# A Mamba/attention trunk on one core: mixer transposes by whole PSUM banks, decay matrices and key-query products for two chunks at once, and a planner that counts a switch between float32r and float32 matmuls

## The chip, the core and the metric

The kernel runs on one core of a Trainium2 chip. The core has a matrix engine (TensorE; PE in the profile, and PEld for its weight loads), a vector engine (VectorE, DVE), a scalar engine (ScalarE, ACT), a general engine (GpSimd, POOL) and a queue engine that mostly starts DMAs (SyncE, SP). Each engine runs its own list of instructions strictly in order and waits for the others through semaphores. Matmuls write to PSUM, eight banks of 512 float32 per partition; GpSimd does not read it here, so results leave PSUM through ACT or DVE.

The metric is the device time of one launch in microseconds (us).

## What is computed

Two layers of a diffusion trunk: a Mamba-2 style mixer (SSD scan, forward and backward) and an attention mixer, over 256 context tokens and 1024 latent tokens, all in float32. The change touches the first mixer only. For each of 8 groups g (4 heads each) and each chunk of 128 tokens it computes, cut to what matters:

```
states = jnp.einsum('bcsgn,bcsgr,bcsgrp->bcgrpn', bc, to_end, xc)        # per chunk, then a scan over chunks
seg    = la_cum[:, :, :, None] - la_cum[:, :, None, :]
decay  = jnp.exp(jnp.where(causal, seg, -jnp.inf))
cb     = jnp.einsum('bclgn,bcsgn->bclsg', cc, bc)                        # key-query product of a chunk
w      = cb[..., None] * decay * dtc[:, :, None]
y_diag = jnp.einsum('bclsgr,bcsgrp->bclgrp', w, xc)
y_off  = jnp.einsum('bclgn,bcgrpn,bclgr->bclgrp', cc, prev, jnp.exp(la_cum))
```

with `xc`, `bc`, `cc` the outputs of an input projection, a 5-tap convolution over tokens and a silu.

## The kernel before

The program has three parts one after another: the mixer (to about 1024 us), the mixer's output projection with the second layer's input projection, and attention. Each part has its own `Plan`: while the program is built, every piece of work is put down with `plan.op(engine, function, after, rank, us, takes, uses)`, and `Plan.order` then plays a list schedule with the written durations `us`. On each engine it starts the ready piece with the lowest rank. The result fixes the order of instructions on every engine; on the chip nothing is reordered. `LINK` (0.5 us) is added when a result goes to another engine. `takes`/`uses` are places in rings of buffers: a piece that takes a place can start when one of the ring's buffers is free in the plan. On the chip the buffers of a ring are handed out in turn, so an instruction waits for the oldest one, whichever the plan had in mind. A piece can name a `table`; a piece whose table differs from the engine's last one gets a penalty on its rank and an extra time. Before, only ACT pieces of the first part name one ("exp", "silu"; changing it loads a function table).

**Projections.** 48 column tiles of 128 (32 for the convolution, 16 for the gate z) over 1280 tokens. For each tile, `load` brings two halves of the weights (`wraw`, SP) and splits them into `whi` (ACT, L599) and `wlo` (POOL or DVE in turn, L602), both float32r. `project` multiplies by blocks of 256, 512 and 512 tokens and 8 steps of 128 rows each; a step is three matmuls into a bank `pj` (helper `mm3`, L168 to L170). `pj` has two banks. `conv_tile` copies them to `ub` (ACT, L636), runs five taps over 1282 tokens (ACT L642, DVE L645 four times, 1.8 us each) and the silu (ACT L650). `z_tile` writes silu(z) (L660) to memory. The tiles go in the order of `ORDER`, each with a rank 10 higher than the one before.

**Mixer of a group** (`mix(g, ...)`, called once the group's four tiles x0, x1, B, C are planned, rank 1 above the last of them, rising by 0.01 per piece). All its matmuls are plain float32.
- `trans`, for each of ten chunks: three transposes (x0, x1, B; L690) into one bank `tc`, of which 384 columns are used; x is copied to `xst` by ACT (L695) or DVE (L697), B to `Bt` by ACT (L701). The ring `tc` has two banks.
- `state`, nine steps: for both directions POOL scales x (`xw`, L713) and PE multiplies it with B into the only bank `st` (L718); POOL decays the state (`tm`, L732), DVE adds (`PV`, L736).
- `wmat`, ten chunks: for both directions SP brings a row of cumulative logs broadcast over partitions (`lab`, 3 buffers, L750), POOL masks it (L754), ACT takes four exponentials (L760) into `W0` or `W1` (two buffers each); DVE adds the two (L773); PE makes the key-query product of the chunk into a bank `tc` (L770), with which DVE multiplies (L775). After each second chunk, PE makes the eight diagonal products into `yd` (L795).
- `inner` adds the skip term (DVE L810); `y_out` makes the products with the earlier states (`yo`, one bank, L837), weights them by `es` (DVE L841; `es` comes by DMA, L832), adds (POOL or DVE, L854) and stores `y_d` (L861).

Beside these, `mod_later` works on the modulation of later parts (DVE L902, L923; PE L935, L936, which also takes `tc` banks).

## Time and profile before

| | |
|---|---|
| median of 3 runs | 2016.39 us (2014.74 to 2016.62) |
| profiled execution | 2017.43 us, of which 2015.7 us is the span from the first to the last instruction |
| granted TensorE clock over the span | 0.993 |
| mixer part | the first projection matmul (L168) starts at 72.7 us, the last one at 1023.0 us |
| instructions of the mixer part's `tc` ring | L690 240 transposes, L770 80 products (160 records: a plain float32 matmul shows as two records) |
| ACT function-table loads in the mixer | L760 58, L660 38, L650 26, 1283 ns each |

The profile names an instruction by engine, line and tiles (`tc<-acc`: written tile, then the ones read). "Idle before" is the engine's idle time ahead of an instruction, put down to what ended it. The end of a matmul is modelled, so two matmul records overlap: 512 columns show as 0.39 us but start 0.23 us apart.

### The profile page before, as it was taken

How to read it: one execution, taken by the hardware profiler on the slowest of the kernel's cores; microseconds unless marked ns; L12 is line 12 of the kernel's file. 1: busy time of each engine (PE TensorE's matmuls, PEld its weight loads, DVE VectorE, ACT ScalarE, POOL GpSimd, SP SyncE). 2: the span in 40 equal slices, each digit the busy share in tenths (PEclk: the TensorE clock that was granted, in tenths of full speed). 3: DMA queues.
4: the chain of work that ended last, by engine and by line, in shares of the span. 5: the costliest groups of instructions: out<-in, count | busy, mean ns of one | idle time of the engine just before them, and what ended most of it. 6: DMA issues, size and time to landing. Idle time of an engine off the chain costs nothing.

```text
span 2015.7 us, 30716 instructions
## 1 busy us (share of the span) xinstructions
PE 1953.1 (97%) x10728; PEld 1498.7 (74%) x10728; DVE 1433.2 (71%) x1737; ACT 1119.5 (56%) x2047; POOL 1189.5 (59%) x973
## 2 busy tenths in 40 slices
PE   8899999999999999999999999999999999999998
PEld 8778888888888788888878878887775444444476
DVE  1475897786959686866545888767675888888643
ACT  2446767666766677676734776543224445454521
POOL 1211776666846576856459787754265667776722
PEclk9989999999999999999999999999999999999999
DMA  6114463635373545455486675462233111111033
GB/s 243 63 32 119 133 188 113 187 98 163 113 198 92 150 131 162 142 142 158 147 280 215 216 252 191 156 179 93 76 91 93 32 38 48 43 43 37 6 104 105
DMA packets 163151, 255.51 MB, mean 127 GB/s; under 512 B 22490, under 2 KB 58202, under 8 KB 162996
## 3 DMA queue, kind: packets, MB, share of 16 engines
q1 hardware_dynamic: 161844, 251.71, 41.2%
q8 instruction: 84, 1.38, 0.3%
q10 hardware_dynamic: 1152, 1.84, 0.2%
q14 instruction: 71, 0.58, 0.1%
HBM read 210.78 MB, written 42.63 MB: 126 GB/s over the span
## 4 chain that ended last, share of the span: by engine, by line
PE 73%; DVE 8%; DMA 7%; POOL 3%; ACT 3%; issue 3%; SPq 2%; DVEq 0%; POOLq 0%; ACTq 0%
PE pj L168 8%; PE pj L169 7%; PE pj L170 7%; PE sc L1663 7%; PE ot L1679 7%; PE ob L168 6%; PE ob L170 6%; PE ob L169 6%; DVE acc L645 3%; PE sc L1462 2%; PE yo L837 2%; PE st L718 2%; DMA spare<-in_mod_w 2%; DMA es<-e_d 2%; PE sc L168 1%
## 5 line engine op out<-in xcount | busy, mean ns | idle before, releaser
L168 PE MATMUL pj<-inh,whi 128*128 128x512 f32 (+1 forms) x1152 | 442.0, 384 | 3.1 <-DVE dv L453 2.4
L169 PE MATMUL pj<-inl,whi 128*128 128x512 f32 (+1 forms) x1152 | 410.2, 356 | 0.8 <-POOL inl L367 0.8
L170 PE MATMUL pj<-inh,wlo 128*128 128x512 f32 (+1 forms) x1152 | 411.0, 357 | 0.0
L168 PEld LDWEIGHTS pj<-inh,whi 128*128 128x128 f32 x1152 | 219.2, 190 | 31.4 <-DVE dv L453 2.8
L170 PEld LDWEIGHTS pj<-inh,wlo 128*128 128x128 f32 x1152 | 218.5, 190 | 32.3
L645 DVE SCALAR_TENSOR_TENSOR acc<-ub,convw,acc 128x1282 f32<-128x1282 f32 x128 | 229.4, 1793 | 17.0 <-ACT acc L642 14.0
L169 PEld LDWEIGHTS pj<-inl,whi 128*128 128x128 f32 x1152 | 219.6, 191 | 26.6 <-POOL inl L367 1.2
L760 ACT ACTIVATE W<-lab,u_t 128x128 f32<-128x128 f32 x640 | 202.7, 391 | 64.6 <-POOL lab L754 42.0
L754 POOL TENSOR_SCALAR_AFFINE_SELECT lab<-lab 128x512 f32<-128x512 f32 x160 | 145.6, 915 | 153.5 <-DMA lab<-la_d 108.6
L1644 POOL TENSOR_TENSOR acc<-acc,P 128x1024 f32<-128x1024 f32 x80 | 192.8, 2411 | 64.1 <-ACT P L1668 62.6
L1668 ACT ACTIVATE P<-sc 128x1024 f32<-128x1024 f32 x160 | 162.9, 1025 | 120.0 <-PE sc L1663 104.4
L1609 DVE TENSOR_REDUCE mx<-sc 128x2 f32<-128x1024 f32 (+1 forms) x140 | 167.4, 1213 | 37.3 <-PE sc L1462 36.4
L713 POOL TENSOR_TENSOR xw<-xst,te_t 128x256 f32<-128x256 f32 x144 | 143.0, 1009 | 41.6 <-PE st L718 17.5
L1679 PE MATMUL ot<-P,vv 128*64 128x512 f32 x640 | 154.7, 605 | 0.0
L602 POOL TENSOR_TENSOR wlo<-wraw,whi 128x512 fp32r<-128x512 f32 x48 | 72.1, 1501 | 121.9 <-ACT whi L599 121.7
L1663 PE MATMUL sc<-q,kh 64*128 64x512 f32 x640 | 136.6, 423 | 4.9 <-DVE qs L1375 2.6
L1663 PEld LDWEIGHTS sc<-q,kh 64*128 64x128 f32 x640 | 60.4, 185 | 74.6 <-DVE mx L1609 29.6
L170 PE MATMUL ob<-whi,yl 128*128 128x512 f32 x288 | 113.4, 394 | 1.8 <-DVE yl L1061 1.4
L168 PE MATMUL ob<-whi,yh 128*128 128x512 f32 x288 | 113.9, 395 | 0.0
L169 PE MATMUL ob<-wlo,yh 128*128 128x512 f32 x288 | 113.0, 392 | 0.0
L902 DVE SCALAR_TENSOR_TENSOR macc<-mraw,cc,macc 128x512 f32<-128x512 f32 x98 | 101.2, 1058 | 11.1 <-DMA mraw<-in_mod_w 10.9
L732 POOL TENSOR_TENSOR tm<-PV,dec_t 128x512 f32<-128x512 f32 x64 | 92.5, 1446 | 17.8 <-DVE PV L736 16.7
(281 smaller groups left out, 4501.8 us busy)
## 6 DMA issues: line engine op xcount, KB each, us to landing
lab<-la_d SPq DMA_DIRECT2D x160, 256.0 KB
wraw<-in_w_in SPq DMA_DIRECT2D x96, 256.0 KB
workvv<-in_m_out_w SPq DMA_DIRECT2D x94, 256.0 KB
mraw<-in_mod_w SPq DMA_DIRECT2D x64, 256.0 KB
es<-e_d SPq DMA_DIRECT2D x128, 128.0 KB
wraw<-in_wqkv SPq DMA_DIRECT2D x48, 256.0 KB
spare<-in_mod_w SPq DMA_DIRECT2D x32, 256.0 KB
q_d<-qs SPq DMA_DIRECT2D x128, 64.0 KB
```

The costliest lines, as they stand in the source:

```text
L168: T.matmul(o, lh, rh, start=first, stop=False)
L169: T.matmul(o, lh, rl, start=False, stop=False)
L170: T.matmul(o, ll, rh, start=False, stop=last)
L645: V.scalar_tensor_tensor(t["a"], ub[i % 2][:, k:k + CW], convw[:, ct, k:k + 1], t["a"], op0=OP.mult, op1=OP.add)
L713: G.tensor_tensor(t[d], s["xst"][:, c], te_t[:, d, c, h4][:, :, None].to_broadcast([128, 4, 64]), op=OP.mult)
L754: G.affine_select(t["l", d], t["l", d], [[0, 4], [sgn, 128]], OP.is_ge, NEVER, base=0, channel_multiplier=-sgn)
L760: S.activation(t["w", d][:, h], t["l", d][:, h], AF.Exp, bias=u_t[:, d, c, 4 * g + h:4 * g + h + 1])
L1609: V.tensor_reduce(max_place(t["m"][0], i), o, AX.X, OP.max)
L1644: E.tensor_tensor(t[e], t["P", k0] if two else t[e], t["P", kt], op=OP.add)
L1663: T.matmul(o[:, h], (first_row[r] if n == 3 else (kh, kl, kh)[n][r, kv, k]), x[(0, 0, 1, 2)[n]][r], start=(n == 0), stop=(n == 3))
L1668: S.activation(t["P", kt], flat(t["s", kt]), AF.Exp)
L1679: T.matmul(t["o"][h * 64:(h + 1) * 64], vv[:, kt, kv], t["P", kt][:, h * 512:(h + 1) * 512], start=(kt == 0), stop=(kt == NT - 1))
```

## The change

It has four pieces, all in the first part.

1. **Transposes by whole banks.** `trans` is called five times instead of ten. It transposes x0 and x1 of two chunks into one bank (512 columns) and copies it at once (ACT for three of the five, DVE for two); B is transposed for four chunks into one bank (the last time two) and copied by ACT at once. `xst` and `Bt` hold the chunks in the order of the transposes, and `at[c]` finds them. The transposes of x no longer wait for the tile B.
2. **Two chunks at once in `wmat`.** It is called for every second chunk. Direction 1 goes first, then direction 0, four exponentials per chunk and direction as before. One DVE addition and one DVE multiplication work on 1024 columns; the two key-query products share a `tc` bank, and the plan starts them only after the third set of four exponentials. `W0` and `W1` hold two chunks and have one buffer each, so the memory is the same and there is no second buffer.
3. **Tables for PE.** In this part the projections name the table "parts" and the mixer's matmuls "whole". The plan charges a change with 4 on the rank and 0.08 us (`plan.switch["PE"]`).
4. **Rings in turn.** For rings named in `ROUND` (here `tc`) the plan gives out a place only if the places before it that share its buffer are free, as the chip does.

The number of matmuls, transposes, exponentials, POOL instructions and DMAs is the same. The order of instructions in the two later parts is the same on every engine.

```diff
+ROUND = ("tc", "y")
...
                     if any(self.free[h.ring] <= i or h.ring not in ANY and h.n != self.given.get(h.ring, 0) + i + 1
-                           for h, i in o.takes):
+                           or h.ring in ROUND and any(x.users for x in out[h.ring][:max(0, len(out[h.ring]) + i + 1 - size[h.ring])]) for h, i in o.takes):
                         continue
-                    r = o.rank + (SWITCH[e][0] if o.table and o.table != table.get(e) else 0.)
+                    r = o.rank + (self.switch[e][0] if o.table and o.table != table.get(e) else 0.)
...
-                 "st": 1, "yd": 1, "yo": 1, "xst": 1, "Bt": 1, "PV": 1, "xw": 3, "tm": 1, "lab": NLAB, "W0": 2, "W1": 2, "es": 3})
+                 "st": 1, "yd": 1, "yo": 1, "xst": 1, "Bt": 1, "PV": 1, "xw": 3, "tm": 1, "lab": NLAB, "W0": 1, "W1": 1, "es": 3})
...
-                               .69 if hi - lo > 256 else .36, takes=[bank] if kt == 0 else [], uses=[bank, w[kt // 4][1]])
+                               .69 if hi - lo > 256 else .36, takes=[bank] if kt == 0 else [], uses=[bank, w[kt // 4][1]], table="parts")
...
-        def trans(n, c):
-            t0, bank, t = tok0(c), plan.hold("tc"), {}
-
-            def turn():
-                t["p"] = psum("tc", [128, 3, 128])
-                for j, x in enumerate((x0, x1, bt)):
-                    T.transpose(t["p"][:, j, :], x["a"][:, t0:t0 + 128], ident)
...
+            def turn(key, tiles, cs):
+                t[key] = psum("tc", [128, len(cs), len(tiles), 128])
+                for i, c in enumerate(cs):
+                    for j, x in enumerate(tiles):
+                        T.transpose(t[key][:, i, j, :], x["a"][:, tok0(c):tok0(c) + 128], ident)
+
+            cs, bank = order[2 * n:2 * n + 2], plan.hold("tc")
+            p = op("PE", lambda: turn("x", (x0, x1), cs), [ax0, ax1, s.get("x")] + third, .45, takes=[bank] + ([] if n else [hxst]),
+                   uses=[hx0, hx1, hxst], table="whole")
+
+            s.setdefault("x", p)
...
-                xd = s["xst"][:, c].rearrange("p h d -> p (h d)")
+                o, i = s["xst"][:, 2 * n:2 * n + 2].rearrange("p c h d -> p (c h d)"), t["x"].rearrange("p c x t -> p (c x t)")
                 if n % 2 == 0:
-                    S.activation(xd, flat(t["p"][:, 0:2]), AF.Copy)
+                    S.activation(o, i, AF.Copy)
                 else:
-                    V.tensor_copy(xd, flat(t["p"][:, 0:2]))
-
-            a = op("PE", turn, [ax0, ax1, ab] + third, .33, takes=[bank] + ([hxst, hBt] if n == 0 else []), uses=[hx0, hx1, hb, hxst, hBt])
-            b = op("DVE" if n % 2 else "ACT", xcopy, [a], .42 if n % 2 else .38, uses=[bank, hxst])
-            d = op("ACT", lambda: S.activation(s["Bt"][:, c, :], t["p"][:, 2, :], AF.Copy), [a], .275, uses=[bank, hBt])
-            ready[c] = (b, d)
...
+            xo = op("DVE" if n % 2 else "ACT", xcopy, [p], .68 if n % 2 else .6, uses=[bank, hxst])
+            if n % 2 == 0:
+                cb, bank2 = order[2 * n:2 * n + 4], plan.hold("tc")
+                p = op("PE", lambda: turn("b", (bt,), cb), [ab, s.get("b")] + third, .11 * len(cb), takes=[bank2] + ([] if n else [hBt]),
+                       uses=[hb, hBt], table="whole")
+                s.setdefault("b", p)
+                d = op("ACT", lambda: S.activation(flat(s["Bt"][:, 2 * n:2 * n + len(cb)]), t["b"].rearrange("p c x t -> p (c x t)"),
+                                                   AF.Copy), [p], .15 * len(cb), uses=[bank2, hBt])
+                for c in cb:
+                    ready[c] = [None, d]
+            for c in cs:
+                ready[c][0] = xo
...
-        def wmat(c):
-                def expo(h, d=d):
-                    if h == 0:
-                        t["w", d] = pool["now"].tile([128, 4, 128], FT, tag=f"W{d}", bufs=2, name="W")
-                    S.activation(t["w", d][:, h], t["l", d][:, h], AF.Exp, bias=u_t[:, d, c, 4 * g + h:4 * g + h + 1])
-                a = op("SP", bring, third + [la_op], .38, takes=[hl])
-                a = op("POOL", close, [a], .88, uses=[hl])
-                for h in range(4):
-                    a = op("ACT", lambda h=h, f=expo: f(h), [a, u_op], .312, takes=[hw] if h == 0 else [], uses=[hl, hw], table="exp")
-                ws.append((hw, a))
...
+        def wmat(c0):
+
+            t, bank, hw = {}, plan.hold("tc"), [plan.hold(f"W{d}") for d in range(2)]
+            done, two = [], (c0, c0 + 1)
+            for d in (1, 0):
+                first = None
+                for k, c in enumerate(two):
+                    hl = plan.hold("lab")
...
+                    def expo(h, d=d, k=k, c=c):
+                        if k == 0 and h == 0:
+                            t["w", d] = pool["now"].tile([128, 2, 4, 128], FT, tag=f"W{d}", bufs=1, name="W")
+                        S.activation(t["w", d][:, k, h], t["l", d, k][:, h], AF.Exp, bias=u_t[:, d, c, 4 * g + h:4 * g + h + 1])
+
+                    a = op("SP", bring, third + [la_op], .38, takes=[hl])
+                    a = op("POOL", close, [a], .88, uses=[hl])
+                    for h in range(4):
+                        a = op("ACT", lambda h=h, f=expo: f(h), [a, u_op, first], .312, takes=[hw[d]] if h == k == 0 else [], uses=[hl, hw[d]],
+                               table="exp")
+                    first = a
+                    done.append(a)
...
             def cross():
-                t["cb"] = psum("tc", [128, 128])
-                T.matmul(t["cb"], bt["a"][:, t0:t0 + 128], ct["a"][:, t0:t0 + 128], start=True, stop=True)
-
-            b = op("PE", cross, [ab, ac], .22, takes=[bank], uses=[hb, hc])
-            a = op("DVE", lambda: V.tensor_tensor(t["w", 0], t["w", 0], t["w", 1], op=OP.add), [w[1] for w in ws], .75,
-                   uses=[w[0] for w in ws])
-            a = op("DVE", lambda: V.tensor_tensor(t["w", 0], t["w", 0], t["cb"][:, None, :].to_broadcast([128, 4, 128]),
-                                                  op=OP.mult), [a, b], .68, uses=[ws[0][0], bank])
...
+                t["cb"] = psum("tc", [128, 2, 128])
+                for k, c in enumerate(two):
+                    T.matmul(t["cb"][:, k], bt["a"][:, tok0(c):tok0(c) + 128], ct["a"][:, tok0(c):tok0(c) + 128], start=True, stop=True)
+
+            def weigh():
+                w = t["w", 0]
+                V.tensor_tensor(w, w, t["cb"][:, :, None, :].to_broadcast([128, 2, 4, 128]), op=OP.mult)
+
+            a = op("DVE", lambda: V.tensor_tensor(t["w", 0], t["w", 0], t["w", 1], op=OP.add), done, 1.3, uses=hw)
+            b = op("PE", cross, [ab, ac, done[2]], .44, takes=[bank], uses=[hb, hc], table="whole")
+            a = op("DVE", weigh, [a, b], 1.22, uses=[hw[0], bank])
...
-                for c, t, _, _ in two:
+                for n, c in enumerate(two):
+            bk["ops"].append(op("PE", diag, [a] + [ready[c][0] for c in two], 1.08, takes=[bk["h"]] if new else [],
+                                uses=[bk["h"], hxst, hw[0]], table="whole"))
...
+    plan.switch["PE"] = (4., .08)
```

What this does to the order of instructions is shown at three places. The lines of the changed kernel are other than before: L172 to L174 are the three projection matmuls (before L168 to L170), L701 the transposes (L690), L743 the state products (L718), L802 the key-query products (L770), L825 the diagonal products (L795), L789 the exponentials (L760).

The first place is PE in the mixer of the third group, at its transposes (`tc<-ident,acc`), with state products and projection steps between them; before:

```order
L690 MATMUL tc<-ident,acc 128x128 x3
L718 MATMUL st<-xw,Bt 128x256 x2
L168 MATMUL pj<-inh,whi 128x512
L169 MATMUL pj<-inl,whi 128x512
L170 MATMUL pj<-inh,wlo 128x512
L690 MATMUL tc<-ident,acc 128x128 x3
```

And in the changed kernel, in the same group:

```order
L701 MATMUL tc<-ident,acc 128x128 x8
L172 MATMUL pj<-inh,whi 128x512
L173 MATMUL pj<-inl,whi 128x512
L174 MATMUL pj<-inh,wlo 128x512
L701 MATMUL tc<-ident,acc 128x128 x4
L743 MATMUL st<-xw,Bt 128x256 x2
L701 MATMUL tc<-ident,acc 128x128 x2
```

One run of three transposes filled one bank; now eight fill two banks, and one projection step stands before the next bank is asked for.

The second place is a little later on PE in the same group, at the first key-query products (`tc<-acc`) and the first diagonal products (`yd<-W,xst`); before:

```order
L770 MATMUL tc<-acc 128x128
L718 MATMUL st<-xw,Bt 128x256 x2
L770 MATMUL tc<-acc 128x128
L168 MATMUL pj<-inh,whi 128x512
L169 MATMUL pj<-inl,whi 128x512
L170 MATMUL pj<-inh,wlo 128x512
L795 MATMUL yd<-W,xst 64x128 x8
L770 MATMUL tc<-acc 128x128
```

And in the changed kernel:

```order
L802 MATMUL tc<-acc 128x128 x2
L172 MATMUL pj<-inh,whi 128x512
L173 MATMUL pj<-inl,whi 128x512
L174 MATMUL pj<-inh,wlo 128x512
L172 MATMUL pj<-inh,whi 128x512
L173 MATMUL pj<-inl,whi 128x512
L174 MATMUL pj<-inh,wlo 128x512
L743 MATMUL st<-xw,Bt 128x256 x2
L172 MATMUL pj<-inh,whi 128x512
L173 MATMUL pj<-inl,whi 128x512
L174 MATMUL pj<-inh,wlo 128x512
L825 MATMUL yd<-W,xst 64x128 x8
```

Before, a third product stood right behind the second one's projection step and the diagonal products; now the two products of a pair stand together, and the diagonal products come three projection steps later, with no further product ahead of them.

The third place is ACT about halfway through the mixer, at the exponentials (`W<-lab,u_t`) of the changed kernel, with what they wait for. The first row is the first exponential into `W0` of a pair:

```order
L789 ACTIVATE W<-lab,u_t 128x128 [waits DVE_49,DMAHW3_49,PE_49,Pool_49]
L789 ACTIVATE W<-lab,u_t 128x128 x3
L603 ACTIVATE whi<-wraw 128x512 [waits DMAHW5_49]
L603 ACTIVATE whi<-wraw 128x512 [waits DMAHW7_49,PE_49]
L640 ACTIVATE ub_110<-pj 128x512 [waits PE_49]
L646 ACTIVATE acc<-ub_110,convw 128x1282 [waits Activation_49]
```

The wait for PE in the first row is for the diagonal products of the pair before, which read the only `W0`; the weight splits and the copy out of the projection's bank stand behind it in ACT's queue.

72 lines of the change are left out of this document (36 added, 36 removed).

## The prediction

> **What bounds the kernel now.** I read the page first, for the engine that the end hangs on, then PE's idle time stretch by stretch, and then who ends it.
>
> ```profile
> PE 1953.1 (97%) x10728; PEld 1498.7 (74%) x10728; DVE 1433.2 (71%) x1737; ACT 1119.5 (56%) x2047; POOL 1189.5 (59%) x973
> PE 73%; DVE 8%; DMA 7%; POOL 3%; ACT 3%; issue 3%; SPq 2%; DVEq 0%; POOLq 0%; ACTq 0%
> ```
>
> PE is busy 97% of the span and carries 73% of the chain that ends last; no other engine passes 71%. The change leaves PE's matmuls as many and as large as they were, so it can only win what PE loses by waiting in the mixer. The stretches (us, then PE's busy time first):
>
> ```profile
> 112.00:1008.00 896.00, 878.60 (x5258) 748.53 (x5259) 678.20 (x783) 618.34 (x1231) 535.24 (x474) 1.00 0.48 139
> 600.00:700.00 100.00, 96.30 (x575) 80.92 (x574) 80.22 (x89) 62.03 (x129) 60.12 (x50) 1.00 0.45 125
> 900.00:1008.00 108.00, 107.95 (x675) 93.03 (x674) 63.59 (x86) 77.28 (x151) 58.30 (x62) 1.00 0.51 152
> 1008.00:1060.00 52.00, 49.03 (x227) 39.34 (x227) 25.56 (x25) 19.64 (x35) 30.18 (x23) 1.00 0.86 281
> ```
>
> From 112 to 1008 us PE is idle for 896 − 878.6 = 17.4 us, most of it in the middle (3.7 us of 600 to 700, next to nothing at the end), and 3.0 us at the passage into the next part. PE's own waits between 112 and 1008 us (waiting line, what ended the wait, us, times, longest):
>
> ```profile
> PE tc L770 <- DVE W L775: 4.9, 6, 1.2
> PE st L718 <- POOL xw L713: 4.9, 5, 2.5
> PE yo L837 <- DVE es L841: 3.2, 6, 1.2
> PE pj L168 <- DVE dv L453: 2.4, 1, 2.4
> PE st L718 <- DVE PV L736: 1.8, 3, 1.2
> PE tc L690 <- DVE xst L697: 0.6, 2, 0.4
> PE tc L690 <- ACT mr L939: 0.6, 1, 0.6
> ```
>
> Without the one at L168, ahead of the mixer, that is 16.0 us in 23 waits. A wait costs a little more than its row says, as PE's row of matmuls shows:
>
> ```profile
> 307.86 0.39 PE L170 MATMUL pj<-inh,wlo 128*128 128x512 f32 x1
> 309.11 0.49 PE L770 MATMUL tc<-acc 128*128 128x128 f32 x2 [0.86 <-DVE W L775]
> ...
> 549.21 0.49 PE L770 MATMUL tc<-acc 128*128 128x128 f32 x2 [1.19 <-DVE W L775]
> 549.63 1.09 PE L795 MATMUL yd<-W,xst 128*64 128x128 f32 x16
> ...
> 670.92 0.28 PE L169 MATMUL pj<-inl,whi 128*128 128x256 f32 x1
> 671.04 0.28 PE L170 MATMUL pj<-inh,wlo 128*128 128x256 f32 x1
> 672.32 0.49 PE L770 MATMUL tc<-acc 128*128 128x128 f32 x2 [1.01 <-DVE W L775]
> 672.65 0.39 PE L837 MATMUL yo<-acc,PV 128*128 128x128 f32 x2
> ```
>
> From 307.86 to 309.11 are 1.25 us where 0.23 us is the usual distance (303.32 to 303.55 below): 1.02 us lost for an idle time of 0.86, so 0.16 us more. With 23 × 0.16 = 3.7 us, the mixer loses 19.7 us to waits. With the 3.0 us behind 1008, a gain over some 23 us has no source in this profile.
>
> **The change, term by term.** The sum is made on the profiled execution (2017.43 us, 1.7 us of it around the span).
>
> *Waits for a `tc` bank* (L770 and L690): 4.9 + 0.6 + 0.6 us in 9 waits, with 9 × 0.16 = 7.5 us. PE asks for the oldest bank while DVE still has to multiply from it. The new plan gives banks in turn, half as many products ask for one, and a product starts only after three of four sets of exponentials; these waits should go. But the diagonal products need the same multiplication. At 549.21 they followed at once (0.42 us later), and the wait would have come there in full. At 309.11 a projection step and state products came between, and at 672.32 a `yo` product followed, no diagonal product; there it would be gone. I take 60%: **−4.5 us** (bounds −7.5 and 0).
>
> *State and `yo` products*: 4.9 + 1.8 + 3.2 us in 14 waits, with 2.2 us 12.1 us. They hang on POOL and DVE being late, and POOL's work stays. DVE and ACT get lighter:
>
> ```profile
> L760 ACT ACT_TABLE_LOAD x58 | 74.4, 1283 | 3.2 <-issue 1.1 <-DVE W L773 0.7 <-DVE W L775 0.5
> L773 DVE TENSOR_TENSOR W<-W 128x512 f32<-128x512 f32 x80 | 69.7, 872 | 39.5 <-ACT W L760 39.1
> L775 DVE TENSOR_TENSOR W<-W,tc 128x512 f32<-128x512 f32 x80 | 54.7, 685 | 3.6 <-PE tc L770 1.4
> L841 DVE TENSOR_TENSOR es<-yo,es 128x512 f32<-128x512 f32 x64 | 43.9, 687 | 50.1 <-DMA es<-e_d 24.5 <-PE yo L837 10.6 <-DMA lab<-la_d 3.5
> L701 ACT ACTIVATE Bt<-tc 128x128 f32<-128x128 f32 x80 | 19.8, 276 | 8.8 <-PE tc L690 5.8 <-DVE xst L697 2.9
> L697 DVE COPY xst<-tc 128x256 f32<-128x256 f32 x40 | 16.1, 415 | 12.7 <-PE tc L690 8.3 <-ACT Bt L701 4.2
> L695 ACT ACTIVATE xst<-tc 128x256 f32<-128x256 f32 x40 | 15.2, 379 | 14.5 <-PE tc L690 14.4
> L725 ACT ACTIVATE PV<-st 128x512 f32<-128x512 f32 x8 | 4.8, 600 | 1.2 <-PE st L718 1.2
> L841 DVE TENSOR_TENSOR es<-yo,es 128x128 f32<-128x128 f32 x32 | 9.2, 287 | 17.7 <-PE yo L837 12.6 <-DMA es<-e_d 4.9
> ```
>
> On DVE 128 columns take 287 ns and 512 take 687, so a column costs 1.04 ns and an instruction 0.154 us by itself. 160 instructions of `W` become 80: 12.3 us less. 40 copies of x become 16 of 512 columns: 16.6 − 16 × 0.687 = 5.6 us less. Together 18 of 678 us. On ACT, 40 copies of x and 80 of B (15.2 + 22.1 us at 379 and 276 ns) become 40 of 512 columns at 600 ns (24 and 16) and 8 of 256 at 379: 27.0 us, 10 us less. The order also has 12 table loads fewer: 15.4 us. None of this is on the chain itself; PE's work covers it, and it only makes DVE and ACT less late where PE waits. Some 3% of load moves waits little: **−1.0 us** of the 12.1 (bounds −6 and +6, half of them either way, since every piece gets another place).
>
> *Fewer switches between projections and mixer.* Runs of mixer matmuls between projections fall from 288 to 224 by the order. The products' durations (minimum, median, maximum in ns), and one switch there and back without a wait:
>
> ```profile
> L770 PE MATMUL tc<-acc x160: 270/273/377, 174.8 to 988.1; 128*128 128x128 f32 x160
> ...
> 303.09 0.39 PE L169 MATMUL pj<-inl,whi 128*128 128x512 f32 x1
> 303.32 0.39 PE L170 MATMUL pj<-inh,wlo 128*128 128x512 f32 x1
> 303.55 0.60 PE L770 MATMUL tc<-acc 128*128 128x128 f32 x4
> 303.91 0.48 PE L168 MATMUL pj<-inh,whi 128*128 128x512 f32 x1
> 304.22 0.40 PE L169 MATMUL pj<-inl,whi 128*128 128x512 f32 x1
> ```
>
> From 303.32 to 304.22 are 0.90 us. Two projection matmuls at 0.23 and four records at 0.11 (the four of L770 last 0.60, the last one alone its median of 0.273) make 0.90: a switch costs about 0.01 us. 64 fewer: **−0.8 us** (bounds −1.5 and 0). The rule meant to keep float32 together does hardly more: its penalty is 4 and the next tile's rank is 10 higher, so ready mixer work still goes first.
>
> *The passage at 1008 to 1060.* In the new order 23 projection steps stand behind the last `yo` product, before 15; at 0.69 us a step the mixer's tail ends 5.5 us earlier against PE's end. But the stores of z hang on the last projections. **−0.5 us** of the 3.0 (bounds −3 and +2).
>
> *A plan that thinks PE slower.* It charges 0.08 us for each of some 448 changes, 36 us that PE will not spend, 4% of 896. PE comes to a mixer product earlier than planned; over a lead that I put at 5 us that is 0.2 us for each of 23 waits: **+1.0 us** (bounds 0 and +4.6).
>
> Sum: −4.5 − 1.0 − 0.8 − 0.5 + 1.0 = −5.8, so 2011.6 us against 2017.43. The median shown (2016.39) lies 1.04 us below that execution: **2010.6 us**.
>
> **Rivals.** *Most waits go* (chance 0.12): all 7.5 us at `tc`, half of the 12.1, 0.8 and the 3.0 at the passage, 17 us: 1999 us. For it speaks that from 900 to 1008 us PE already runs without waits at a similar load.
>
> *The waits change places* (0.26): DVE's late multiplication stops PE at L795 instead, as at 549, and POOL's is late as before. 0 to −3 us: 2013 to 2016.
>
> *The wide additions hold up POOL* (0.05).
>
> ```profile
> L773 DVE TENSOR_TENSOR W<-W x80: 672/693/1790, 198.9 to 999.2; 128x512 f32<-128x512 f32 x80
> L713 POOL TENSOR_TENSOR xw<-xst,te_t x144: 603/1042/1889, 204.5 to 964.5; 128x256 f32<-128x256 f32 x144
> ```
>
> The addition (minimum, median, maximum in ns) takes from 672 to 1790 and POOL's scaling from 603 to 1889, while DVE's multiplication from PSUM stays at 685: where DVE and POOL both read SBUF, one waits for the other. An addition of 1024 columns lasts 0.672 + 512 × 1.04 ns = 1.2 us, so POOL waits on average 0.6 us for it instead of 0.34, in half as many places: 40 × 1.2 × 0.6 − 80 × 0.672 × 0.336 = 10.7 us at most, 6 us at POOL's share of 0.6. If all of it reached PE through `xw`, the gain would be used up: 2016 us. The Trainium skill, page "SBUF — State Buffer", section "SBUF: two separate sides", says that such an addition and a GpSimd instruction reading SBUF shut each other out for a whole instruction. The rows just shown agree with that rule.
>
> *The single `W0` blocks ACT* (0.13), the slow side.
>
> ```profile
> ACT W L760 <- PE yd L795: 19.9, 12, 4.7
> ...
> L760 ACT ACTIVATE W<-lab,u_t 128x128 f32<-128x128 f32 x640 | 202.7, 391 | 64.6 <-POOL lab L754 42.0 <-PE yd L795 19.9 <-issue 1.8
> ```
>
> Already with two buffers ACT waits 19.9 us for diagonal products, once 4.7 us. With one, each of 40 pairs waits for the pair before, and behind that exponential ACT's queue holds the copy out of `pj`. A 256-token block takes eight steps of three matmuls at 0.12 us (670.92 to 671.04), 2.9 us; if ACT stands longer than that, PE has no free `pj` bank. Ten such pairs at 1.5 us cost 15 us: 2025 us. Against it: five pairs in a group's 100 us leave 20 us for a chain of some 10 us (16 exponentials at 0.39, 1.2 + 1.2 on DVE, 1.1 on PE).
>
> **How the numbers follow.** The forecast has 0.44 (its own range 2004 to 2014), the rivals 0.12, 0.26, 0.05 and 0.13. Differences under 0.2% (4.0 us) can't be told from no change here. Faster than 2012.4: 0.40 of the forecast and 0.12 = 0.52. Same: 0.04 + 0.24 + 0.04 = 0.32; slower 0.16. The range 1997 to 2022 leaves out the far ends of the fast and the slow rival, some 0.15; its lower end is the fast rival with 2 us more, its upper end lies within the slow one.
>
> **What would show it.** In the profile of the changed kernel: no wait at the key-query products (L802), and shorter new ones at L825; state and `yo` waits near 12 us; table loads 12 fewer; between 112 and 1008 us PE idle near 13 us. Waits at projections (L172) behind ACT's copies would make the slow rival right; PE idle of 17 us with L825 in the list, the second one; and a distance over 0.95 us where 0.90 stands above, a switch dearer than I read it.

## The result and the profile after

| | before | after |
|---|---|---|
| median of six runs each | 2015.97 us (2011.57 to 2018.80) | 2027.63 us (2023.40 to 2028.71) |
| profiled execution, its span | 2017.43, 2015.7 us | 2028.56, 2026.8 us |
| first transpose of the mixer | 202.2 us | 179.0 us |
| last `yo` product | 1013.3 us | 1018.8 us |
| last projection matmul | 1023.4 us | 1033.6 us |

The ratio of the times is 1.0052, 95% interval 1.0038 to 1.0065: the changed kernel is half a per cent slower. 10.2 of the 11.1 us by which its span is longer are there when the last projection is done, so the mixer part is the place. The first group's mixer work starts 23 us earlier and still the last `yo` product comes 5.5 us later.

The page's busy times and chain of the changed kernel:

```profile
PE 1951.7 (96%) x10728; PEld 1500.2 (74%) x10728; DVE 1422.6 (70%) x1633; ACT 1099.0 (54%) x1963; POOL 1204.3 (59%) x973
PE 64%; DVE 8%; DMA 3%; ACT 3%; issue 2%; POOL 1%; SPq 1%; DVEq 0%; ACTq 0%; POOLq 0%
```

PE's busy time is the same within 1.4 us, so the added time is idle time. By stretches (us, then PE, PEld, DVE, ACT and POOL busy, the granted clock, DMA), first of the changed kernel:

```profile
112.00:1008.00 896.00, 867.16 (x5188) 740.12 (x5188) 660.46 (x669) 591.45 (x1137) 550.12 (x473) 0.99 0.48 138
200.00:300.00 100.00, 92.07 (x572) 77.52 (x570) 86.76 (x84) 69.45 (x140) 74.57 (x59) 1.00 0.51 144
300.00:400.00 100.00, 94.35 (x564) 80.61 (x563) 68.22 (x72) 69.09 (x132) 55.66 (x51) 1.00 0.55 154
600.00:700.00 100.00, 96.00 (x575) 81.76 (x574) 77.83 (x78) 62.15 (x125) 67.65 (x55) 0.98 0.46 129
900.00:1008.00 108.00, 107.82 (x669) 92.69 (x668) 64.47 (x71) 74.53 (x142) 67.26 (x64) 1.00 0.55 165
1008.00:1060.00 52.00, 49.45 (x244) 40.73 (x243) 21.97 (x26) 18.08 (x33) 21.46 (x18) 0.97 0.74 247
```

From 112 to 1008 us PE now idles 28.8 us, before 17.4. The stretches where before it hardly waited have become the worst, with 7.9 us idle of 200 to 300 and 5.7 us of 300 to 400 (2.4 and 1.6 us before); at the end it still runs without waits. DVE and ACT give no reason by their busy time, which is lower than before, and the clock gives none either: over the whole span 0.993 was granted in both kernels. PE's own waits in the mixer part (waiting line, what ended the wait, us, times, longest):

```profile
PE st L743 <- DVE PV L762: 13.0, 15, 2.1
PE yo L867 <- DVE es L871: 8.2, 6, 2.5
PE yd L825 <- DVE W L806: 2.8, 5, 1.5
PE tc L701 <- ACT Bt L722: 2.7, 1, 2.7
PE st L743 <- POOL xw L738: 1.1, 2, 0.9
PE tc L802 <- DVE xst L714: 0.7, 1, 0.7
PE st L743 <- ACT PV L751: 0.2, 1, 0.2
```

The waits for a `tc` bank behind DVE's multiplication are gone. PE waits instead behind the state's addition (13.0 us, before 1.8) and the `es` product (8.2, before 3.2), two instructions that the change did not touch. One such wait, in the timeline of all engines (start, length, engine, line):

```profile
208.34 3.21 DVE L932 SCALAR_TENSOR_TENSOR macc<-mraw,cc,macc 128x512 f32<-128x512 f32 x3
...
208.90 1.13 PE L743 MATMUL st<-xw,Bt 128*128 128x256 f32 x4
...
211.48 0.86 DVE L840 SCALAR_TENSOR_TENSOR acc<-acc,dskip,yd 128x256 f32<-128x256 f32 x2
...
211.85 0.28 PE L174 MATMUL pj<-inh,wlo 128*128 128x256 f32 x1
...
212.26 0.67 DVE L762 TENSOR_TENSOR PV<-tm,st 128x512 f32<-128x512 f32 x1
...
212.99 1.13 PE L743 MATMUL st<-xw,Bt 128*128 128x256 f32 x4 [0.85 <-DVE PV L762]
```

The addition that frees the only `st` bank has its place on DVE behind three background updates (3.21 us) and two skip terms. PE is through its four projection steps at 212.1, while DVE, which has not paused since 208.34, gets to the addition only at 212.26. DVE works without a pause while PE stands: in the order this addition has its place too late for a PE of this speed.

### The profile page after: what moved, and what is told of

Read it like the earlier page. It is cut to its first block, busy times and chain, and to the rows that moved or that the text cites. A ratio compares the mean times of both kernels' runs of the same rounds, so it can differ in the third digit from the quotient of the medians.

```text
span 2026.8 us, 30474 instructions
## 1 busy us (share of the span) xinstructions
PE 1951.7 (96%) x10728; PEld 1500.2 (74%) x10728; DVE 1422.6 (70%) x1633; ACT 1099.0 (54%) x1963; POOL 1204.3 (59%) x973
## 4 chain that ended last, share of the span: by engine, by line
PE 64%; DVE 8%; DMA 3%; ACT 3%; issue 2%; POOL 1%; SPq 1%; DVEq 0%; ACTq 0%; POOLq 0%
PE sc L1694 7%; PE ot L1710 7%; PE ob L172 6%; PE ob L174 6%; PE ob L173 6%; PE pj L172 5%; PE pj L173 5%; PE pj L174 5%; DVE acc L649 3%; PE yo L867 2%; PE sc L1493 2%; PE st L743 2%; PE sc L172 1%; PE sc L174 1%; PE sc L173 1%
## 5 line engine op out<-in xcount | busy, mean ns | idle before, releaser
L172 PE MATMUL pj<-inh,whi 128*128 128x512 f32 (+1 forms) x1152 | 436.5, 379 | 3.9 <-DVE dv L457 3.2
L174 PE MATMUL pj<-inh,wlo 128*128 128x512 f32 (+1 forms) x1152 | 410.4, 356 | 0.0
L649 DVE SCALAR_TENSOR_TENSOR acc<-ub,convw,acc 128x1282 f32<-128x1282 f32 x128 | 230.6, 1801 | 18.3 <-ACT acc L646 14.8
L172 PEld LDWEIGHTS pj<-inh,whi 128*128 128x128 f32 x1152 | 219.1, 190 | 32.6 <-DVE dv L457 3.6
L174 PEld LDWEIGHTS pj<-inh,wlo 128*128 128x128 f32 x1152 | 218.3, 190 | 31.9
L789 ACT ACTIVATE W<-lab,u_t 128x128 f32<-128x128 f32 x640 | 202.1, 390 | 61.5 <-POOL lab L783 37.9
L783 POOL TENSOR_SCALAR_AFFINE_SELECT lab<-lab 128x512 f32<-128x512 f32 x160 | 157.7, 992 | 116.3 <-DMA lab<-la_d 99.8
L738 POOL TENSOR_TENSOR xw<-xst,te_t 128x256 f32<-128x256 f32 x144 | 152.4, 1075 | 35.7 <-PE st L743 23.2
L871 DVE TENSOR_TENSOR es<-yo,es 128x512 f32<-128x512 f32 (+1 forms) x96 | 53.1, 553 | 101.1 <-DMA es<-e_d 47.3
L758 POOL TENSOR_TENSOR tm<-PV,dec_t 128x512 f32<-128x512 f32 x64 | 96.8, 1512 | 36.3 <-DVE PV L762 36.2
L174 PE MATMUL ob<-whi,yl 128*128 128x512 f32 x288 | 113.4, 394 | 1.8 <-DVE yl L1092 1.8
L172 PE MATMUL ob<-whi,yh 128*128 128x512 f32 x288 | 114.1, 396 | 0.0
```

The lines of the kernel that those rows point to most:

```text
L172: T.matmul(o, lh, rh, start=first, stop=False)
L174: T.matmul(o, ll, rh, start=False, stop=last)
L649: V.scalar_tensor_tensor(t["a"], ub[i % 2][:, k:k + CW], convw[:, ct, k:k + 1], t["a"], op0=OP.mult, op1=OP.add)
L738: G.tensor_tensor(t[d], s["xst"][:, at[c]], te_t[:, d, c, h4][:, :, None].to_broadcast([128, 4, 64]), op=OP.mult)
L783: G.affine_select(t["l", d, k], t["l", d, k], [[0, 4], [sgn, 128]], OP.is_ge, NEVER, base=0, channel_multiplier=-sgn)
L789: S.activation(t["w", d][:, k, h], t["l", d, k][:, h], AF.Exp, bias=u_t[:, d, c, 4 * g + h:4 * g + h + 1])
```

## The experiments

Four theories stood against each other. **The charge**: the plan reckons with 0.08 us at each change between projections and mixer, the chip needs about 0.01, so the order is made for a slower PE. **The pairs**: two chunks of `W` at once make DVE, ACT and POOL work in larger lumps. **The banks**: transposes by whole banks tie the start of a group to two or four chunks. **Scatter** ("replan" in the expectations): any edit gives another order, and orders differ by some 10 us without a cause. In the expectations the charge is called "price".

To compare orders I add up, from the 300th to the last projection matmul of the mixer, how much longer than usual the step from one matmul to the next is where the trace shows PE idle between them; this is called "waits" below (before 21.1 us in 29 places, after 34.6 in 35). Without its waits that stretch is 848 to 855 us long in every kernel, while the waits go from 8.3 to 34.6 us, so the waits are most of the difference. They are read from one profiled execution of each kernel, and that execution lies up to 5 us off the kernel's median (e7's was its slowest, e8's its fastest). "Runs" are the uninterrupted runs of mixer matmuls between projections, counted in the order. The ratios are against the kernel before, timed again with each set on the same chip; e1 to e4, e5 to e8 and e9 to e12 were each timed together.

| kernel | median us | ratio (95%) | waits us / places | runs |
|---|---|---|---|---|
| after | 2027.63 | 1.0052 (1.0038 to 1.0065) | 34.6 / 35 | 224 |
| e1: after, charge 0 | 2008.98 | 0.9974 (0.9960 to 0.9988) | 17.8 / 25 | 228 |
| e2: after, old `wmat` | 2029.96 | 1.0086 (1.0063 to 1.0108) | 31.2 / 52 | 244 |
| e3: after, old `trans` | 2028.44 | 1.0073 (1.0048 to 1.0099) | 30.2 / 36 | 240 |
| e4: before, rings in turn | 2010.51 | 0.9981 (0.9965 to 0.9998) | 14.8 / 24 | 278 |
| e5: before, tables and charge | 2024.31 | 1.0050 (1.0035 to 1.0065) | 29.8 / 38 | 267 |
| e6: charge 0, steps planned 4.5% longer | 2019.82 | 1.0024 (1.0014 to 1.0034) | 28.9 / 38 | 246 |
| e7: after, charge 0 and penalty 0 | 2009.56 | 0.9977 (0.9968 to 0.9987) | 18.2 / 27 | 257 |
| e8: after, charge 0.01 | 2007.95 | 0.9966 (0.9954 to 0.9977) | 15.1 / 23 | 231 |
| e9: after, all but PE planned 4.5% slower | 2001.76 | 0.9931 (0.9916 to 0.9946) | 11.8 / 19 | 222 |
| e10: charge 0.01, DVE and POOL as measured | 2000.54 | 0.9929 (0.9914 to 0.9944) | 8.3 / 11 | 229 |
| e11: after, charge 0.04 | 2018.69 | 1.0017 (1.0004 to 1.0029) | 25.5 / 30 | 231 |
| e12: e7 without rings in turn | 2013.93 | 0.9996 (0.9984 to 1.0008) | 23.0 / 29 | 259 |

### e1 to e4: which piece

**e1**, the change without its charge:

```diff
-    plan.switch["PE"] = (4., .08)
+    plan.switch["PE"] = (4., 0.)
```

> The changed kernel with one number altered: the plan charges no time for a PE switch between projections and mixer (the rank penalty of 4 stays). Theory 'price' (the plan thinks PE slower by 0.08 us at some 448 switches, so PE reaches the mixer's products earlier than planned and waits there): about 2016 us, PE's waits in the mixer back from 28.7 to some 16 us. Theory 'pairs' (two chunks at once make DVE's state additions and the es loads late): stays at 2024 to 2030 us, with waits of state products for DVE L762 near 13 us and of yo near 8. Theory 'replan' (every new order scatters by some 10 us, whatever the reason for it): anywhere from 2010 to 2030.

Measured 2008.98 us, ratio 0.9974. PE's busy time from 112 to 1008 us and its waits in this kernel:

```profile
112.00:1008.00 896.00, 882.24 (x5319) 754.70 (x5318) 675.77 (x685) 599.68 (x1149) 565.19 (x478) 1.00 0.47 142
```

```profile
PE st L743 <- DVE PV L762: 5.3, 7, 1.5
PE yd L825 <- DVE W L806: 3.3, 6, 1.0
PE yo L867 <- DVE es L871: 1.8, 3, 1.1
PE tc L701 <- DVE xst L714: 1.7, 2, 1.4
PE st L743 <- POOL xw L738: 1.0, 1, 1.0
```

One number, which no instruction of the kernel contains, turns a loss of 0.5% into a gain of 0.3%; the time is 7 us under the 2016 us expected of the charge theory. PE's idle time falls from 28.8 to 13.8 us, and what falls are the waits at the two lines that had grown (13.0 to 5.3 and 8.2 to 1.8).

**e2**, the change with the decay matrices one chunk at a time, as before (two buffers of `W0` and `W1`), and the charge kept:

```diff
-        def wmat(c0):
+        def wmat(c):
...
-            a = op("DVE", lambda: V.tensor_tensor(t["w", 0], t["w", 0], t["w", 1], op=OP.add), done, 1.3, uses=hw)
-            b = op("PE", cross, [ab, ac, done[2]], .44, takes=[bank], uses=[hb, hc], table="whole")
-            a = op("DVE", weigh, [a, b], 1.22, uses=[hw[0], bank])
...
+            b = op("PE", cross, [ab, ac], .22, takes=[bank], uses=[hb, hc], table="whole")
+            a = op("DVE", lambda: V.tensor_tensor(t["w", 0], t["w", 0], t["w", 1], op=OP.add), [w[1] for w in ws], .75,
+                   uses=[w[0] for w in ws])
```

> The changed kernel with the decay matrices one chunk at a time as before (512-column additions and multiplications, two buffers each for W0 and W1, one key-query product per bank); the transposes by whole banks, the PE tables and the rings in turn stay. Theory 'pairs': back to 2013 to 2018 us, waits for DVE L762's state addition and for es under 8 us together. Theory 'price': stays over 2023 us. Theory 'replan': anywhere from 2010 to 2030.

Measured 2029.96 us, ratio 1.0086: the pairs are not the cause. Without them the loss is no smaller, and the waits for a `tc` bank behind DVE's multiplication are back (8.7 us in 12 places).

**e3**, the change with the transposes three per chunk, as before, and the charge kept:

```diff
-        def trans(n):
+        def trans(n, c):
...
+                t["p"] = psum("tc", [128, 3, 128])
+                for j, x in enumerate((x0, x1, bt)):
+                    T.transpose(t["p"][:, j, :], x["a"][:, t0:t0 + 128], ident)
...
-        for n in range(NT // 2):
-            trans(n)
+        for n, c in enumerate(order):
+            trans(n, c)
```

> The changed kernel with the transposes three at a time per chunk as before; the decay matrices for two chunks, the PE tables and the rings in turn stay. Theories 'price' and 'pairs': both 2023 us and more. A theory 'banks' (the transposes by whole banks, and their earlier start, are what costs): about 2016 us. Theory 'replan': anywhere from 2010 to 2030.

Measured 2028.44 us, ratio 1.0073: the banks are not the cause either.

**e4**, the kernel before with the rule on rings alone:

```diff
+ROUND = ("tc", "y")
...
-                           for h, i in o.takes):
+                           or h.ring in ROUND and any(x.users for x in out[h.ring][:max(0, len(out[h.ring]) + i + 1 - size[h.ring])]) for h, i in o.takes):
```

> The kernel before with the rings in turn alone (the plan gives a tc bank only when the older holder of its buffer is done). By the prediction's first term: the 7.5 us of waits for tc banks shrink to 3 or less and the time falls to about 2011 us. Theory 'replan': the waits move to other lines, and the time lies anywhere from 2008 to 2026.

Measured 2010.51 us, ratio 0.9981. The time is as expected, the way there is not: the waits at `tc` are still 5.9 us (before 6.1), and the gain came at the state and `yo` products (4.5 us, before 9.9). A rule on one ring moved the whole order.

### e5 to e8: the charge without the rest, and other ways to a slow PE

**e5**, the kernel before with the tables and the charge alone:

```diff
-                               .69 if hi - lo > 256 else .36, takes=[bank] if kt == 0 else [], uses=[bank, w[kt // 4][1]])
+                               .69 if hi - lo > 256 else .36, takes=[bank] if kt == 0 else [], uses=[bank, w[kt // 4][1]], table="parts")
...
-            b = op("PE", cross, [ab, ac], .22, takes=[bank], uses=[hb, hc])
+            b = op("PE", cross, [ab, ac], .22, takes=[bank], uses=[hb, hc], table="whole")
...
+    plan.switch["PE"] = (4., .08)
```

> The kernel before with the PE tables alone (projections 'parts', mixer 'whole', penalty 4 and 0.08 us per change of table in the plan); transposes, decay matrices and rings as before. Theory 'price': 2024 us or more and 28 us or more of PE waits in the mixer, with nothing else of the change in it. Theory 'replan': anywhere from 2008 to 2030. If it stays at 2010 to 2016 us, 'price' needs another piece of the change to act.

Measured 2024.31 us, ratio 1.0050. PE's waits in it:

```profile
PE tc L771 <- DVE W L776: 8.3, 12, 1.4
PE yo L838 <- DVE es L842: 7.4, 8, 1.8
PE st L719 <- POOL xw L714: 3.5, 5, 0.8
PE st L719 <- DVE PV L737: 3.5, 7, 1.0
PE tc L691 <- ACT Bt L702: 0.6, 1, 0.6
```

The charge costs the old code as much as the whole change does. Three of the four larger waits of before are longer and in more places: 8.3 us in 12 where the product waits for DVE's multiplication, before 4.9 in 6; `yo` 7.4 (3.2 before) and the state's addition 3.5 (1.8). The fourth, for POOL's `xw`, is shorter (3.5, before 4.9). So the charge has no line of its own: in the old code it lengthens other waits than in the changed one.

**e6**, no charge, but each projection step planned at 0.72 us instead of 0.69 (0.375 instead of 0.36 for 256 tokens), which also makes PE about 4% slower in the plan alone:

```diff
-                               .69 if hi - lo > 256 else .36, takes=[bank] if kt == 0 else [], uses=[bank, w[kt // 4][1]], table="parts")
+                               .72 if hi - lo > 256 else .375, takes=[bank] if kt == 0 else [], uses=[bank, w[kt // 4][1]], table="parts")
...
-    plan.switch["PE"] = (4., .08)
+    plan.switch["PE"] = (4., 0.)
```

> The changed kernel with no time for a switch, but with each projection step planned 4% too long (0.72 and 0.375 us for 0.69 and 0.36; the trace has 0.68 and 0.36), some 36 us over the mixer, as much as 448 switches at 0.08. Theory 'price' in its general form (a plan in which PE is slower than on the chip puts products too early for DVE and the es loads): 2022 us or more. If only the switch as such mattered: about 2009, as without its time. Theory 'replan': anywhere from 2005 to 2030.

Measured 2019.82 us, ratio 1.0024. Against e1 it loses 0.5%, and 11 us of waits. The direction is that of the charge theory, but the 2022 us or more that it expected were not reached: the loss against e1 is some two thirds of the charge's.

**e7**, no charge and no penalty, so that the order takes no notice of the two kinds of matmul:

```diff
-    plan.switch["PE"] = (4., .08)
+    plan.switch["PE"] = (0., 0.)
```

> The changed kernel with neither penalty nor time for a switch on PE: the tables have no effect, float32 work is not kept together. 'Price': about 2009 us, as with the penalty alone. If the penalty's grouping (fewer runs of mixer work) is worth something by itself: 3 us or more above 2009. 'Replan': scatter of 10 us.

Measured 2009.56 us, ratio 0.9977, beside e1's 0.9974. The penalty takes 257 runs to 228, and the time can't be told apart: keeping float32 work together buys nothing that can be measured here.

**e8**, the charge at what the trace showed:

```diff
-    plan.switch["PE"] = (4., .08)
+    plan.switch["PE"] = (4., .01)
```

> The changed kernel with 0.01 us per switch in the plan, what the trace of before shows (0.90 us where the sum of the matmuls is 0.89 to 0.90). 'Price': 2009 to 2012 us. 'Replan': an order that differs a little from the one with no time scatters anywhere from 2005 to 2028.

Measured 2007.95 us, ratio 0.9966, as good as no charge and 1 us under the range expected.

### e9 to e12: too slow against what, and a better plan

**e9** keeps the 0.08 us and makes everything else in the plan 4.5% slower too: the other engines' durations, the time from engine to engine and the transfers.

```diff
-                us = o.us
+                us = o.us * (1. if e in ("PE", "-") else self.slow)
...
-    plan.switch["PE"] = (4., .08)
+    plan.switch["PE"], plan.slow = (4., .08), 1.045
```

> The changed kernel as it is, 0.08 us per switch included, but in the mixer's plan the other engines' durations, the time between engines and the landing of DMAs are 4.5% longer too, so that PE is no longer slow in relation to them. Theory 'price' in its relative form: the loss is undone, 2008 to 2014 us, PE waits in the mixer under 20 us. If the charge at single switches misleads the plan locally (which product goes where), whatever the other engines' pace: 2023 us or more.

Measured 2001.76 us, ratio 0.9931. With the charge of the slow kernel in place, this one is faster than all of e1 to e8. PE's three longest waits in the mixer:

```profile
PE st L744 <- DVE PV L763: 6.1, 6, 1.4
PE yo L868 <- DVE es L872: 1.2, 3, 0.6
PE yd L826 <- DVE W L807: 0.9, 4, 0.3
```

So it is not the 0.08 us as such that harm, but their ratio to what the plan thinks of the others. The time is also 6 us under the 2008 us at which the expected range begins. That it even beats e1 suggests that without a charge the plan still took the others for too fast.

**e10** takes that up: a charge of 0.01, and eight durations of DVE and POOL as the profile of the changed kernel has them. Five of the nine changed numbers:

```diff
-            a = plan.op("DVE", lambda k=k: tap(k), [a], rank - URGENT, 1.70, uses=[u, out])
+            a = plan.op("DVE", lambda k=k: tap(k), [a], rank - URGENT, 1.80, uses=[u, out])
...
-                a = op("POOL", scale, [ready[c][0], te_op], .80, takes=[hw], uses=[hxst])
+                a = op("POOL", scale, [ready[c][0], te_op], 1.05, takes=[hw], uses=[hxst])
...
-                a = op("POOL", decay, [pv[0]] + dec_ops, 1.11, takes=[ht], uses=[hPV])
+                a = op("POOL", decay, [pv[0]] + dec_ops, 1.48, takes=[ht], uses=[hPV])
...
-                done[0] = plan.op("DVE", lambda j=j, f=add: f(j), [a, done[0]], rank, .92, uses=[raw])
+                done[0] = plan.op("DVE", lambda j=j, f=add: f(j), [a, done[0]], rank, 1.06, uses=[raw])
...
-    plan.switch["PE"] = (4., .08)
+    plan.switch["PE"] = (4., .01)
```

> The changed kernel with 0.01 us per switch and with the plan's costs of DVE and POOL pieces set to what the changed kernel's profile shows (taps 1.80 for 1.70, macc 1.06 for 0.92, addition of 1024 columns 1.45 for 1.3, xw 1.05 for 0.80, tm 1.48 for 1.11, mask 0.95 for 0.88, wlo on DVE 0.94 for 0.80, the one-row macc 1.1 for 0.70). 'Price': waits for DVE and POOL shrink further, from 15 us to under 10, 2000 to 2005 us. If what is left comes from the DMAs' landing instead: 2006 to 2010.

Measured 2000.54 us, ratio 0.9929 (0.9914 to 0.9944): faster than both kernels. PE's busy time from 112 to 1008 us and its waits:

```profile
112.00:1008.00 896.00, 889.51 (x5348) 763.98 (x5349) 677.89 (x687) 615.17 (x1166) 571.40 (x481) 1.00 0.48 143
```

```profile
PE tr L172 <- ACT yh L1087: 5.5, 1, 5.5
PE tc L701 <- DVE xst L714: 1.8, 2, 1.0
PE st L743 <- DVE PV L762: 1.7, 3, 0.7
PE yo L867 <- DVE es L871: 1.2, 2, 1.0
PE tc L701 <- ACT Bt L722: 1.2, 1, 1.2
PE yd L825 <- DVE W L806: 0.3, 1, 0.3
```

PE idles 6.5 of 896 us, and the waits of the mixer are 6.2 us. What is left is one wait of 5.5 us at L172 (`tr`), which lies behind the mixer, in the passage into the next part: in this profile the last projection starts 19 us earlier than before (1004 instead of 1023 us), and what follows it takes 5.9 us longer.

**e11**, the charge halved:

```diff
-    plan.switch["PE"] = (4., .08)
+    plan.switch["PE"] = (4., .04)
```

> The changed kernel with half the charge, 0.04 us per switch. 'Price' as a dose: between 2009 (0 and 0.01) and 2027.6 (0.08), about 2014 to 2020 us, waits 20 to 28 us. 'Replan': no order in it.

Measured 2018.69 us, ratio 1.0017. The four charges 0, 0.01, 0.04 and 0.08 gave the ratios 0.9974, 0.9966, 1.0017 and 1.0052. The plan's bill for them (two changes a run) is 0, 4.6, 18.5 and 35.8 us; against e1 the last two lose 0.43% and 0.78% of 2016 us, 8.7 and 15.7 us. So in the changed kernel nearly half of what the plan charges comes back as time, except at the smallest charge. In the old code (e5, 267 runs) it is a quarter, 10.1 of 42.7 us.

**e12**, the transposes by banks and the pairs alone, with neither tables nor the rule on rings:

```diff
-ROUND = ("tc", "y")
+ROUND = ()
...
-    plan.switch["PE"] = (4., .08)
+    plan.switch["PE"] = (0., 0.)
```

> The changed kernel with neither the PE tables (no penalty, no time) nor the rings in turn: only transposes by whole banks and the decay matrices for two chunks. With the rings in turn it took 2009.6. If the rings in turn bring the 4 us that they brought alone: 2013 to 2015, with waits at L701 or L802 for tc banks; if half as many products on the ring make the rule idle: 2009 to 2011.

Measured 2013.93 us, ratio 0.9996 (0.9984 to 1.0008). The two pieces that change instructions are together worth nothing that can be told from no change; the rule on rings looks worth some 0.2% on top of them (e7 against e12, whose intervals just overlap), as on the old code (e4). But the waits for `tc` banks that were expected of a kernel without the rule aren't there: 0.6 us in e12, 0.7 us in e7.

**What falls.** Scatter: the four kernels with the full charge and nothing set against it (after, e2, e3, e5) took 2024 to 2030 us, the six with a charge of 0.01 or none and all other durations as the plan had them (before, e1, e4, e7, e8, e12) 2008 to 2016; half the charge lies between. Different orders within each set differ by some 6 to 8 us, which is what scatter there is, and it doesn't reach across. Pairs and banks fall with e2, e3 and e5: without either the loss stays, and without both it is there too. The charge stands, in the sharper form that e9 gives it: the plan's ratio of PE's time to that of the others counts.

## Why the prediction was wrong, step by step

**The step that failed: "A plan that thinks PE slower", +1.0 us.** The mechanism was named, the sign was right, and even the bill (36 us, 4% of 896) was worked out; the size was wrong. The runs give 0.78% between after and e1, 15.7 us (18.7 between the medians, which were not timed together). I priced the charge at 0.2 us for each wait that the trace of before showed, 4.6 us at most, and took less than a quarter of that. The error lies in the count and in the lead: the rows of waits show only those products that were late already, and many others had just enough time. The trace of before shows it for the state products. Of the 71 steps behind the first, 6 start within 0.15 us of the end of the addition (or copy) that frees the `st` bank, and 35 more within 1 us of it; in the changed kernel 18 start within 0.15 us. With the charge there are 35 waits instead of e1's 25, and each lasts 0.99 us on average instead of 0.71; split up so, the difference of 16.8 us is 10 more waits (10 × 0.99) and 25 longer ones (25 × 0.28). A lead of 5 us was my choice and rested on no row. The bill itself, 36 us, would have been the safer bound: the loss stayed under the bill at every charge (15.7 of 35.8, 8.7 of 18.5, 10.1 of 42.7 in e5). That it can't exceed it is an argument, which these runs don't prove.

Without this step's error the sum comes out near, in part by luck: the terms other than the plan's make −6.8 us, and e1 measured −0.26%, −5.2 us (−8.1 to −2.4). "Between 112 and 1008 us PE idle near 13 us" is what e1 shows (13.8). But of the 5.5 us by which waits were to shrink, e1's profile shows 3.3 (21.1 to 17.8), and not where they were forecast.

**Waits for a `tc` bank, −4.5 us.** The waits behind DVE's multiplication went, as "no wait at the key-query products" said (only 0.7 us behind a copy of x stands at L802). And as it said, some turned up at the diagonal products: 2.8 us at L825 (3.3 in e1, 2.6 in e12). Another `tc` wait of 2.7 us, ahead of a transpose, is new. Idle time at `tc` and at the diagonal products together went from 6.1 to 6.2 us after, and to 5.0 in e1: nearer to the rival "the waits change places" than to 60%. This term was too large by some 3 us. What the kernel without the charge gained goes with the order rather than with the wider instructions: e4 gains as much with the old ones (0.9981), and e12, with the new ones alone, gains nothing that can be measured (0.9996).

**State and `yo` products, −1.0 us.** DVE and ACT got lighter, but less than was worked out. The groups of the changed kernel in the mixer part (count, busy us, mean ns, idle ahead and its releasers):

```profile
L789 ACT ACTIVATE W<-lab,u_t 128x128 f32<-128x128 f32 x640 | 202.1, 390 | 61.5 <-POOL lab L783 37.9 <-issue 15.9 <-DVE W L808 6.0
L808 DVE TENSOR_TENSOR W<-W 128x1024 f32<-128x1024 f32 x40 | 58.0, 1451 | 22.3 <-ACT W L789 22.2
L806 DVE TENSOR_TENSOR W<-W,tc 128x1024 f32<-128x1024 f32 x40 | 48.7, 1218 | 2.4
L789 ACT ACT_TABLE_LOAD x52 | 66.7, 1283 | 13.2 <-PE yd L825 8.0 <-issue 2.8 <-DVE W L806 1.6
L712 ACT ACTIVATE xst<-tc 128x512 f32<-128x512 f32 x24 | 14.2, 593 | 20.2 <-PE tc L701 20.1
L714 DVE COPY xst<-tc 128x512 f32<-128x512 f32 x16 | 10.9, 682 | 8.4 <-PE tc L701 8.4
L738 POOL TENSOR_TENSOR xw<-xst,te_t 128x256 f32<-128x256 f32 x144 | 152.4, 1075 | 35.7 <-PE st L743 23.2 <-ACT xst L712 10.0 <-DVE xst L714 1.3
L758 POOL TENSOR_TENSOR tm<-PV,dec_t 128x512 f32<-128x512 f32 x64 | 96.8, 1512 | 36.3 <-DVE PV L762 36.2
```

`W` takes 106.7 us of DVE instead of 124.4, which is more saved than forecast. But over the whole execution DVE's busy time falls by 10.6 us only (1433.2 to 1422.6; 18 forecast), since other instructions got longer, and ACT's by 20.5 (1119.5 to 1099.0; 25 forecast with the table loads, of which there are 12 fewer, as forecast). The windows of 112 to 1008 us mislead here: they show 17.7 and 26.9 us less, in part because the changed kernel has done less of its work by 1008 us. The waits did not follow: state and `yo` waits are 22.5 us after, 8.1 in e1, before 9.9. The half per cent lies in these lines, and the charge put it there; without it the forecast of a little less holds.

**Fewer switches, −0.8 us.** 288 runs became 224, and a switch costs no more than was read. PE's row in the changed kernel:

```profile
326.25 0.28 PE L174 MATMUL pj<-inh,wlo 128*128 128x256 f32 x1
326.37 1.02 PE L743 MATMUL st<-xw,Bt 128*128 128x256 f32 x4
327.24 0.61 PE L802 MATMUL tc<-acc 128*128 128x128 f32 x4
327.60 0.37 PE L172 MATMUL pj<-inh,whi 128*128 128x256 f32 x1
327.80 0.28 PE L173 MATMUL pj<-inl,whi 128*128 128x256 f32 x1
```

From L802's start to the second projection matmul are 0.56 us, four records at 0.11 and one projection matmul of 256 columns at 0.12. Ahead of 512 columns, nine such places of this kernel show 0.677 us in the median, 0.01 more than 4 × 0.11 + 0.228. The plan paid 0.08 twice for this. "The rule does hardly more" was wrong in the count (it alone takes 257 runs to 228, e7 and e1) and right in the time.

**The passage, −0.5 us.** PE idles 2.55 us between 1008 and 1060, before 2.97, and as much in the 52 us that lie 10.2 us later, where this kernel's passage is. The time from the last projection to the end didn't fall: 993.2 us, before 992.3. No gain can be seen.

**The rivals.** "The single `W0` blocks ACT" foresaw a slow kernel, but for another reason: its sign, waits at L172 behind ACT's copies, isn't there. Ahead of the table loads at L789 ACT stands 8.0 us for diagonal products, where with two buffers it stood 19.9 at L760; another 15.9 us ahead of the exponentials (1.8 before) have no releaser in the profile. "The wide additions hold up POOL" is true of the engines: the addition takes 1.45 us on average where 1.2 was worked out, and POOL as a whole is busy 14.8 us longer. In the profiles of all ten kernels with wide additions POOL is busy 1204 to 1228 us, in the four with narrow ones (before, e2, e4, e5) 1181 to 1197. It is not the cause of the loss, since in e1 and e10 the additions are as wide, and those kernels are faster.

**What stays open.** Why the waits of this order fall on the state's addition and on `es`. The timeline above shows DVE busy with planned-too-short background updates ahead of the addition (1.07 us each, 0.92 in the plan), and e10, which corrects these, leaves 1.7 us at this line; but e10 corrects eight costs at once, and none was tried alone. PE's own work between one state step and the next may have become shorter in the order: the projection matmuls between them, at 0.228 or 0.12 us each, make in the median 2.1 us after, 2.5 in e1 and 2.8 in e10, but 2.1 in e7, which is as fast as e1. So a simple count of projection steps ahead of a product doesn't show it. Nor was it tried whether the charge would harm a plan whose other costs are right.

## What to carry to other kernels

In a kernel whose order comes from a list schedule with written durations, a change to a cost is a change to the program: measure the cost from a trace before it is entered, and give every engine's costs the same care, since their ratio decides. When an edit makes the plan's time for the bounding engine longer than its real one, bound the loss by the whole surplus, under which it stayed in every run here, and not by the waits that the old profile shows, because products with just enough time don't show there. Here the two pieces that rewrote instructions were worth nothing measurable by themselves (e12), while nine corrected numbers of the plan made of a kernel that lost 0.5% one that gains 0.7%.

## What the hardware showed beside this

- A change from float32r to plain float32 matmuls and back costs PE about 0.01 us here (0.677 us where the matmuls' own distances make 0.668), so little that grouping them (257 runs or 228) does not show in the time (e7, e1).
- DVE's addition of 1024 columns from SBUF takes 1451 ns on average beside 1218 ns for the multiplication of the same width from PSUM. Two additions of 512 columns took 2 × 872 ns, so widening saved 0.29 us a piece.
- Several of POOL's instructions got longer by no edit of their own: `xw` from 1009 ns on average to 1075, the state's decay (`tm`) from 1446 to 1512, the mask (`lab`) from 915 to 992, and POOL's busy time by 14.8 us.
